# Second expert table of the last stage loaded in pieces of 512 rows by 512 columns, and six row buffers

## The chip, the core and the metric

One NeuronCore of one Trainium2 chip runs the whole program. The engines are TensorE (PE, matrix products), VectorE (DVE), ScalarE (ACT), GpSimd (POOL) and SyncE (SP), which work at the same time and wait for each other through semaphores. 16 DMA engines move data between HBM and the on-chip memory; SP issues the plain transfers, POOL the gathers by index. The metric is the time of one execution in microseconds, median of the runs.

## What is computed

One step of a decoder layer for 1024 prompt tokens and 64 sample tokens: three attention-like branches, then a layer of product-key experts (PEER), then a norm. The last stage concerns PEER alone: 16384 experts, each a row of 1024 values in the tables `peer_u` and `peer_v`; each token uses 8 x 16 of them.

```python
def peer_ffn(xn, w_pq, k1, k2, u_tab, v_tab):
    ...
    eidx = jnp.take_along_axis(cidx, pos, axis=-1)
    g = jax.nn.softmax(sc, axis=-1)
    ...
        a = jax.nn.gelu(jnp.einsum('td,thkd->thk', xb, u_tab[ib]).astype(jnp.float32))
        return jnp.einsum('thk,thkd->td', (gb * a).astype(v_tab.dtype), v_tab[ib])
```

All inputs and outputs are float32.

## The kernel before

The tokens are nine blocks of up to 128 (eight of the prompt, number 8 with the 64 sample tokens). Each block's experts are computed in one of two ways.

*Gathered blocks* (0 to 3, 6 and 7; `peer_gather`). For each of the 128 experts of a token POOL issues a gather of one row per token, 128 rows of 4 KB, 512 KB together, into a row buffer: 128 gathers of U rows (L1097) and 128 of V rows (L1108) for a block. DVE multiplies a U row with the token and sums (L1099, two instructions on DVE), and adds a weighted V row to the block's sum (L1114). U rows of head h+1 come before V rows of head h. The row buffers are taken in turn by `big`, and a gather waits until the row that last lay in its buffer is used up. In the last stage there are `ROWS2` of them: `ROWS` = 4 that are always there, and the others in the pool `dn` of the last stage.

*Dense blocks* (4, 5 and the sample block 8, 320 tokens together; `peer_dense`). Both tables are read whole, in 16 groups of DG = 8 slices of 128 experts. For each slice the U rows are loaded (L1218, 512 KB, tile `dur`), transposed on PE (L1223), split in a high part (ACT, L1225, `duh`) and a low part (DVE, L1226, `dul`), and 24 products of 320 columns give the activations (L1244 to L1247, `pa`). They become expert weights by a gelu and a product with the choice of each token (L1251, tile `c8`), and are split again (`dwh` on L1254, `dwl` on L1255). When a group's eight slices are done, eight *turns* follow, one for each 128 of the 1024 output columns: the V values of 1024 experts by 128 columns are loaded (L1259, 512 KB, tile `dvr`, two buffers), split (`dvh` on ACT, L1262; `dvl` on DVE, L1263), multiplied in 24 products (L1267 to L1269, `py`), and added to the sum `yT` on DVE (L1273). There are twelve weight buffers (DW), so that slices of the next group can run beside the turns of this one.

The gathers of blocks 6 and 7 run in the same stage as the dense blocks. The order of each engine's instructions is made when the program is built, by a list scheduler that goes by priorities and its own estimate of times; the gathers have the lowest priority and fill what it takes for gaps. On the chip this order is fixed: an engine waits at an instruction until its inputs are there. After the last turn each dense block is transposed back and normed (`finish`), and block 7 is finished when its last V row is added.

The functions that the change touches, and what calls them:

## Time and profile before

| | |
|---|---|
| median of 3 runs | 4262.14 us (4254.17 to 4282.94) |
| profiled execution | 4270.01 us, its span 4268.2 us |
| PE busy | 3480.7 us (82% of the span) |
| DVE busy | 3300.5 us (77%) |
| POOL busy | 2053.5 us (48%) |
| ACT busy | 1513.1 us (35%) |
| DMA | 1285.50 MB, mean 301 GB/s |
| gathers issued by POOL | 768 of U rows, 768 of V rows |

Busy time counts the stretches in which an engine had an instruction running; products on PE are pipelined, and their ends are modelled. In names of the trace the tiles of the last stage begin with d (`dvr`, `dur`, `duh`), and `in_peer_v_dram` is the V table in HBM. A wait is put down to what came last. PE's granted clock is given as a share of 2.4 GHz, and 0.5 is its lower level of 1.2 GHz.

### The profile page before, as it was taken

Reading aid. Unit: us, or ns where it says so; the run is one execution under the profiler, and the core shown is the slowest. Engines: PE = TensorE matmul, PEld = TensorE weight load, DVE = VectorE, ACT = ScalarE, POOL = GpSimd, SP = SyncE. Lnnn points to the kernel's source line nnn. Section 1 sums busy time; section 2 is a strip of 40 time slices with the busy share of each in tenths; the row PEclk is TensorE's granted clock in tenths of the full one; section 3 lists DMA queues with packets and bytes.
Section 4 is the critical chain, followed back from the end, with each engine's and each line's share of the span. In section 5 each row is a group of like instructions: output and inputs, shape, how many; then the busy total and the mean of one; then the engine's idle time right before and its main releaser. Section 6 shows DMA issues by size and latency. Waiting matters only on the chain.

```text
span 4268.2 us, 57773 instructions
## 1 busy us (share of the span) xinstructions
PE 3480.7 (82%) x19287; PEld 2867.8 (67%) x19287; DVE 3300.5 (77%) x7763; ACT 1513.1 (35%) x3138; POOL 2053.5 (48%) x1722
## 2 busy tenths in 40 slices
PE   4999895879967698587878877675589999898884
PEld 4989694656645557365655554453589999898884
DVE  3444368787787789888886656679999998898898
ACT  2565542324244112244464422111533333332331
POOL 0000003556656555665665667564344554555556
PEclk9999897989969898787888998887799999999997
DMA  3334346989989999898998899998899999999998
GB/s 114 109 96 146 122 158 205 321 287 344 368 278 372 361 354 312 308 321 283 365 322 312 329 328 353 381 370 304 323 348 331 341 357 357 359 355 363 335 353 300
DMA packets 690128, 1285.50 MB, mean 301 GB/s; under 512 B 66685, under 2 KB 447509, under 8 KB 687270
## 3 DMA queue, kind: packets, MB, share of 16 engines
q0 software_dynamic: 230480, 839.23, 53.4%
q1 hardware_dynamic: 459350, 442.58, 31.7%
q8 instruction: 153, 2.51, 0.2%
q14 instruction: 145, 1.19, 0.1%
HBM read 1213.04 MB, written 68.59 MB: 300 GB/s over the span
## 4 chain that ended last, share of the span: by engine, by line
PE 31%; DVE 16%; DMA 10%; issue 8%; ACT 3%; POOL 3%; another core or an unknown queue 1%; SPq 0%; POOLq 0%; DVEq 0%; ACTq 0%
DVE u L1099 5%; PE pj L272 4%; DVE acc L1114 4%; PE pa L1244 2%; PE pa L1245 2%; PE py L1269 2%; PE pj L275 2%; PE pa L1247 2%; PE py L1267 2%; PE py L1268 2%; DMA dvr<-in_peer_v_dram 2%; PE pt L1223 2%; DMA u<-in_peer_u_dram,ei 1%; POOL u L1097 1%; DMA v<-in_peer_v_dram,ei 1%
## 5 line engine op out<-in xcount | busy, mean ns | idle before, releaser
L1097 POOL DMA_INDIRECT u<-in_peer_u_dram,ei x768 | 972.2, 1266 | 796.9 <-DVE a L1099 191.5
L1108 POOL DMA_INDIRECT v<-in_peer_v_dram,ei x768 | 944.4, 1230 | 726.7 <-DVE acc L1114 285.2
L1114 DVE SCALAR_TENSOR_TENSOR acc<-v,a,acc 128x1024 f32<-128x1024 f32 x762 | 978.4, 1284 | 22.0 <-DMA v<-in_peer_v_dram,ei 14.6
L1099 DVE CUSTOM_DVE_ANT_0 u<-u,x 128x1024 f32<-128x1024 f32 x768 | 924.4, 1223 | 65.4 <-DMA u<-in_peer_u_dram,ei 61.7
L272 PE MATMUL pj<-aT,wr 128*128 128x384 f32 (+1 forms) x1664 | 530.4, 473 | 13.3 <-issue 5.2
L272 PEld LDWEIGHTS pj<-aT,wr 128*128 128x128 f32 x1664 | 317.6, 196 | 179.5 <-issue 19.6
L1267 PE MATMUL py<-dwh,dvh 128*128 128x320 f32 x1024 | 329.7, 324 | 55.1 <-ACT dwh L1254 32.3
L1269 PE MATMUL py<-dwh,dvl 128*128 128x320 f32 x1024 | 331.2, 324 | 42.7 <-DVE dvl L1263 42.7
L275 PE MATMUL pj<-wr,aT 128*128 128x256 f32 x1344 | 318.6, 395 | 22.5 <-DVE z L920 17.3
L1268 PE MATMUL py<-dwl,dvh 128*128 128x320 f32 x1024 | 328.1, 321 | 0.0
L1244 PE MATMUL pa<-xh,duh 128*128 128x320 f32 x1024 | 309.5, 315 | 6.6 <-ACT duh L1225 4.8
L275 PEld LDWEIGHTS pj<-wr,aT 128*128 128x128 f32 x1344 | 261.4, 198 | 65.4 <-DVE z L920 18.9
L1245 PE MATMUL pa<-xl,duh 128*128 128x320 f32 x1024 | 304.9, 310 | 0.0
L1225 ACT ACTIVATE duh<-pt 128x512 fp32r<-128x512 f32 x256 | 148.2, 597 | 382.9 <-PE pt L1223 347.0
L1267 PEld LDWEIGHTS py<-dwh,dvh 128*128 128x128 f32 x1024 | 203.4, 199 | 58.1 <-ACT dwh L1254 32.6
L1269 PEld LDWEIGHTS py<-dwh,dvl 128*128 128x128 f32 x1024 | 203.0, 198 | 49.0 <-DVE dvl L1263 49.0
L281 DVE TENSOR_TENSOR wl<-wr,wh 128x512 fp32r<-128x512 f32 x200 | 137.8, 691 | 123.3 <-PE pj L291 42.5
L1268 PEld LDWEIGHTS py<-dwl,dvh 128*128 128x128 f32 x1024 | 203.4, 199 | 0.3 <-DVE dwl L1255 0.3
L1244 PEld LDWEIGHTS pa<-xh,duh 128*128 128x128 f32 x1024 | 192.5, 188 | 11.2 <-ACT duh L1225 8.5
L1247 PE MATMUL pa<-xh,dul 128*128 128x320 f32 x1024 | 195.7, 320 | 0.0
L1245 PEld LDWEIGHTS pa<-xl,duh 128*128 128x128 f32 x1024 | 192.7, 188 | 0.0
L1226 DVE TENSOR_TENSOR dul<-pt,duh 128x512 fp32r<-128x512 f32 x256 | 171.9, 689 | 19.5 <-ACT duh L1225 17.4
(503 smaller groups left out, 7067.7 us busy)
## 6 DMA issues: line engine op xcount, KB each, us to landing
wr<-in_w_in_dram SPq DMA_DIRECT2D x168, 512.0 KB
dvr<-in_peer_v_dram SPq DMA_DIRECT2D x128, 512.0 KB
dur<-in_peer_u_dram SPq DMA_DIRECT2D x128, 512.0 KB
wr<-in_w_pq_dram SPq DMA_DIRECT2D x48, 512.0 KB
dc<-c_scr SPq DMA_DIRECT2D x15, 1280.0 KB
c_scr<-stg SPq DMA_DIRECT2D x16, 1024.0 KB
wr<-in_w_out_dram SPq DMA_DIRECT2D x24, 512.0 KB
u<-in_peer_u_dram,ei POOLq DMA_INDIRECT x768
```

Of the source, the lines that this page charges most:

```text
L272: PE.matmul(ps, raw[:, i, cols[0] * 128:cols[0] * 128 + 128], x[:, k], start=k == 0, stop=k == kt - 1)
L275: PE.matmul(ps, x[:, k, :], raw[:, i], start=k == 0 and first, stop=k == kt - 1 and last)
L1097: G.indirect_dma_start(out=r, out_offset=None, in_=UR, in_offset=bass.IndirectOffsetOnAxis(ap=ei[:, s:s + 1], axis=0))
L1099: V.tensor_tensor_reduce(r, r, x2, 1.0, 0.0, OP.mult, OP.add, a[:, s:s + 1])
L1108: G.indirect_dma_start(out=r, out_offset=None, in_=VR, in_offset=bass.IndirectOffsetOnAxis(ap=ei[:, s:s + 1], axis=0))
L1114: V.scalar_tensor_tensor(acc, r, a[:, s:s + 1], acc, op0=OP.mult, op1=OP.add)
L1244: PE.matmul(pa[:, :NT], uh[:, k], xh[:, k], start=k == 0, stop=False)
L1245: PE.matmul(pa[:, :NT], uh[:, k], xl[:, k], start=False, stop=False)
L1247: PE.matmul(pa[:, :NT], ul[:, k], xh[:, k], start=False, stop=k == 7)
L1267: PE.matmul(py[:, :NT], vh[:, j], wh, start=j == 0, stop=False)
L1268: PE.matmul(py[:, :NT], vh[:, j], wl, start=False, stop=False)
L1269: PE.matmul(py[:, :NT], vl[:, j], wh, start=False, stop=j == DG - 1)
```

## The change

The V table comes in pieces of 512 experts by 512 columns (tile `v4`, 1 MB, three buffers). Two pieces, of the first and of the last four slices, serve four turns; they are loaded at turns 0 and 4. A turn splits its 128 columns out of both pieces, with two instructions of half the size on ACT and on DVE each. A run of consecutive bytes in a load is 2 KB instead of 512 bytes. The tile `vr` is left with one buffer, for the end of the dense blocks. The last stage has six row buffers instead of eight.

```diff
--- before.py
+++ after.py
@@ -37,7 +37,7 @@
 OFF = [sum(NB[:a]) for a in range(16)]
 NCAND = sum(NB)
 
-ROWS, MORE, ROWS2 = 4, 3, 8
+ROWS, MORE, ROWS2 = 4, 3, 6
 SAMPLE = 8
 GROUPS = [[0, 1, 2], [3, 4, 5], [SAMPLE, 6, 7]]
 
@@ -1180,7 +1180,7 @@
 
 
         pd = ctx2.enter_context(tc.tile_pool(name="pd", bufs=1, space=bass.MemoryType.PSUM))
-        DB = {"ur": 3, "uh": 2, "ul": 2, "w": 4, "wh": DW, "wl": DW, "c": 2, "hot": 7, "eg": 1, "vr": 2, "vh": 2, "vl": 2}
+        DB = {"ur": 3, "uh": 2, "ul": 2, "w": 4, "wh": DW, "wl": DW, "c": 2, "hot": 7, "eg": 1, "v4": 3, "vr": 1, "vh": 2, "vl": 2}
         PB = {"t": 2, "a": 2, "y": 2, "c": 2}
 
         def DT(tag, shape, dt=F32):
@@ -1255,12 +1255,19 @@
                 V.tensor_tensor(wl, w, wh.bitcast(F32), op=OP.subtract)
                 W.append((wh, wl))
             for dt_ in range(8):
-                v = DT("vr", [128, DG, 128])
-                SP.dma_start(v, VR[g * DG * 128:(g + 1) * DG * 128, dt_ * 128:(dt_ + 1) * 128].rearrange(
-                    "(j p) d -> p j d", p=128))
+
+                if dt_ % 4 == 0:
+                    v4 = [DT("v4", [128, DG // 2, 512]) for _ in range(2)]
+                    for i, v in enumerate(v4):
+                        r = (g * DG + i * DG // 2) * 128
+                        SP.dma_start(v, VR[r:r + DG * 64, dt_ * 128:dt_ * 128 + 512].rearrange(
+                            "(j p) d -> p j d", p=128))
                 vh, vl = DT("vh", [128, DG, 128], F32R), DT("vl", [128, DG, 128], F32R)
-                A.activation(vh, v, AF.Copy)
-                V.tensor_tensor(vl, v, vh.bitcast(F32), op=OP.subtract)
+                for i, v in enumerate(v4):
+                    js = slice(i * DG // 2, (i + 1) * DG // 2)
+                    x = v[:, :, dt_ % 4 * 128:dt_ % 4 * 128 + 128]
+                    A.activation(vh[:, js], x, AF.Copy)
+                    V.tensor_tensor(vl[:, js], x, vh[:, js].bitcast(F32), op=OP.subtract)
                 py = DP("y")
                 for j in range(DG):
                     wh, wl = W[j]
```

The order of instructions changes with it, in the last stage alone. Two places show it.

On DVE, at the end of the dense blocks. Before, from the second-last update of `yT` on (L1273; L1114 adds a V row of block 7, L1073 and L1079 finish a dense block):

```order
L1273 TENSOR_TENSOR yT<-yT,py_34528 128x320
L1114 SCALAR_TENSOR_TENSOR acc_22963<-v_23595,a_22860,acc_22963 128x1024
L1114 SCALAR_TENSOR_TENSOR acc_22963<-v_23598,a_22860,acc_22963 128x1024
L1273 TENSOR_TENSOR yT<-yT,py_34560 128x320
L1114 SCALAR_TENSOR_TENSOR acc_22963<-v_23601,a_22860,acc_22963 128x1024
L1073 TENSOR_TENSOR dvr_34588<-dvr_34588,dur_34589 128x1024
L1114 SCALAR_TENSOR_TENSOR acc_22963<-v_23604,a_22860,acc_22963 128x1024
L1073 TENSOR_TENSOR dvr_34611<-dvr_34611,dur_34612 128x1024
L1114 SCALAR_TENSOR_TENSOR acc_22963<-v_23607,a_22860,acc_22963 128x1024
L1079 SCALAR_TENSOR_TENSOR dvr_34588<-dvr_34588,fr_34606,dur_34586 128x1024
```

Behind the last of these updates stand 15 instructions of L1114 in all, and none of L1099. With the change, from the second-last update of `yT` on, which is L1280 there:

```order
L1280 TENSOR_TENSOR yT<-yT,py_34656 128x320
L1114 SCALAR_TENSOR_TENSOR acc_22963<-v_23256,a_22860,acc_22963 128x1024
L1280 TENSOR_TENSOR yT<-yT,py_34688 128x320
L1102 TENSOR_TENSOR a_22860<-a_22860,gw_21819 128x16
L1114 SCALAR_TENSOR_TENSOR acc_22963<-v_23259,a_22860,acc_22963 128x1024
L1073 TENSOR_TENSOR dvr_34716<-dvr_34716,dur_34717 128x1024
L1114 SCALAR_TENSOR_TENSOR acc_22963<-v_23262,a_22860,acc_22963 128x1024
L1114 SCALAR_TENSOR_TENSOR acc_22963<-v_23265,a_22860,acc_22963 128x1024
L1114 SCALAR_TENSOR_TENSOR acc_22963<-v_23268,a_22860,acc_22963 128x1024
L1079 SCALAR_TENSOR_TENSOR dvr_34716<-dvr_34716,fr_34734,dur_34714 128x1024
L1114 SCALAR_TENSOR_TENSOR acc_22963<-v_23271,a_22860,acc_22963 128x1024
L1114 SCALAR_TENSOR_TENSOR acc_22963<-v_23274,a_22860,acc_22963 128x1024
```

Behind the last update there now stand 79 V rows (L1114) and 48 U rows (L1099, 96 instructions); ahead of it, from the first expert weight on, stand 181 U rows and 177 V rows, which were 224 and 240.

On SP, in the middle of the stage, the loads of U slices (`dur`, L1218) and of the V table before (`dvr`, L1259):

```order
L1218 DMA dur_26760<-in_peer_u_dram 128x1024
L1259 DMA dvr_26452<-in_peer_v_dram 128x8x128
L1218 DMA dur_26810<-in_peer_u_dram 128x1024
L1259 DMA dvr_26484<-in_peer_v_dram 128x8x128
L1235 DMA dc_27366<-c_scr 128x20x128
L1218 DMA dur_26860<-in_peer_u_dram 128x1024
L1259 DMA dvr_26516<-in_peer_v_dram 128x8x128
L1218 DMA dur_26910<-in_peer_u_dram 128x1024
L1259 DMA dvr_26548<-in_peer_v_dram 128x8x128
```

and with the change (a piece `v4` is printed as `dv` with a number, L1263):

```order
L1263 DMA dv_5949_27143<-in_peer_v_dram 128x4x512
L1263 DMA dv_5962_27274<-in_peer_v_dram 128x4x512
L1218 DMA dur_27092<-in_peer_u_dram 128x1024
L1218 DMA dur_27408<-in_peer_u_dram 128x1024
L1218 DMA dur_27458<-in_peer_u_dram 128x1024
L1218 DMA dur_27508<-in_peer_u_dram 128x1024
L1235 DMA dc_28072<-c_scr 128x20x128
L1218 DMA dur_27558<-in_peer_u_dram 128x1024
L1218 DMA dur_27608<-in_peer_u_dram 128x1024
L1263 DMA dv_5963_27275<-in_peer_v_dram 128x4x512
L1263 DMA dv_6049_27808<-in_peer_v_dram 128x4x512
```

Where a V load stood behind nearly every U load, two pieces of 1 MB now stand together after two to five U loads. At the stage's start three pieces stand ahead of the U loads, where two loads of `dvr` stood.

## Rows read from the trace of the kernel before

**Rows 1.** The page's head, its first part (busy time, share of the span and number of instructions of each engine) and, from the part with the costliest groups, four of them: line, engine, operation, out<-in with shapes, count | busy us, mean ns of one | idle time before and what ended it.
```profile
span 4268.2 us, 57773 instructions
PE 3480.7 (82%) x19287; PEld 2867.8 (67%) x19287; DVE 3300.5 (77%) x7763; ACT 1513.1 (35%) x3138; POOL 2053.5 (48%) x1722
...
L1097 POOL DMA_INDIRECT u<-in_peer_u_dram,ei x768 | 972.2, 1266 | 796.9 <-DVE a L1099 191.5
L1108 POOL DMA_INDIRECT v<-in_peer_v_dram,ei x768 | 944.4, 1230 | 726.7 <-DVE acc L1114 285.2
L1114 DVE SCALAR_TENSOR_TENSOR acc<-v,a,acc 128x1024 f32<-128x1024 f32 x762 | 978.4, 1284 | 22.0 <-DMA v<-in_peer_v_dram,ei 14.6
L1099 DVE CUSTOM_DVE_ANT_0 u<-u,x 128x1024 f32<-128x1024 f32 x768 | 924.4, 1223 | 65.4 <-DMA u<-in_peer_u_dram,ei 61.7
```

**Rows 2.** Busy time by stretch: from:to in us, length, then busy us and number of instructions of PE, PE's weight loads, DVE, ACT and POOL, then granted clock of TensorE, busy share of the DMA engines and GB/s.
```profile
3104.00:4230.00 1126.00, 1032.31 (x6966) 1014.16 (x6966) 1036.19 (x1755) 378.88 (x652) 584.47 (x468) 0.95 0.98 350
4230.00:4268.00 38.00, 1.56 (x10) 0.93 (x10) 28.47 (x24) 6.76 (x12) 17.72 (x16) 0.56 0.62 208
3150.00:3400.00 250.00, 242.66 (x1685) 239.01 (x1684) 245.76 (x586) 93.95 (x160) 116.81 (x91) 0.99 0.98 342
3600.00:4230.00 630.00, 549.23 (x3616) 537.77 (x3614) 564.42 (x799) 189.38 (x321) 346.77 (x279) 0.92 0.98 353
4150.00:4230.00 80.00, 53.05 (x290) 50.51 (x288) 71.00 (x88) 13.69 (x17) 57.38 (x45) 0.79 0.99 354
```

**Rows 3.** DVE in order of time at the end of the program: start us, us, line, operation, out<-in with shapes, how many in a row.
```profile
4229.57 0.49 DVE L1273 TENSOR_TENSOR yT<-yT,py 128x320 f32<-128x320 f32 x1 [0.95 <-PE py L1269]
...
4242.62 7.88 DVE L1114 SCALAR_TENSOR_TENSOR acc<-v,a,acc 128x1024 f32<-128x1024 f32 x6
...
4260.03 1.22 DVE L1073 TENSOR_TENSOR acc<-acc,h 128x1024 f32<-128x1024 f32 x1
```

**Rows 4.** What PE waited for from 3104 to 4230 us, the three largest: line, releaser: total us, times, longest us.
```profile
PE py L1269 <- DVE dvl L1263: 42.7, 21, 5.7
PE py L1267 <- ACT dwh L1254: 32.3, 1, 32.3
PE py L1267 <- ACT dvh L1262: 22.2, 8, 7.6
```

**Rows 5.** PE in order of time, at two places: start us, us, line, operation, and in brackets the idle time before it and what ended it. The first row is the first product with an expert weight, the two others are the first and the last of four products in a row at full clock.
```profile
3104.43 0.90 PE L1267 MATMUL py<-dwh,dvh 128*128 128x320 f32 x2 [32.30 <-ACT dwh L1254]
...
4139.51 0.31 PE L1268 MATMUL py<-dwl,dvh 128*128 128x320 f32 x1
...
4139.95 0.31 PE L1268 MATMUL py<-dwl,dvh 128*128 128x320 f32 x1
```

**Rows 6.** What ACT waited for from 3104 to 4230 us, one row.
```profile
ACT dvh L1262 <- DMA dvr<-in_peer_v_dram: 133.8, 32, 12.4
```

**Rows 7.** The chain of work that ended last, in order of time, one load of a V piece: start us, us, what.
```profile
3476.20 18.91 DMA dvr<-in_peer_v_dram
```

**Rows 8.** SyncE's queue in order of time, the two loads that it issued there.
```profile
3475.26 0.34 SPq L1218 DMA_DIRECT2D dur<-in_peer_u_dram  x1
3476.20 0.37 SPq L1259 DMA_DIRECT2D dvr<-in_peer_v_dram  x1
```

**Rows 9.** Busy time from 3104 to 4230 us of the instructions of one line alone (same columns as in group 2, for the engines that have any), for L1099 (u rows, two instructions each), L1114 (v rows) and L1223 (transposes of the U table).
```profile
3104.00:4230.00 1126.00, 271.29 (x448) 0.95 0.98 350
3104.00:4230.00 1126.00, 307.16 (x240) 0.95 0.98 350
3104.00:4230.00 1126.00, 138.21 (x952) 116.11 (x952) 0.95 0.98 350
```

**Rows 10.** DMA queues from 3100 to 4200 us: packets, MB, and the time that their packets took as a share of 16 engines over the stretch. q0 carries the gathers that POOL issues, q1 what SyncE issues.
```profile
q0 software_dynamic: 64811, 236.01, 56.9%
q1 hardware_dynamic: 181809, 147.87, 40.9%
```

**Rows 11.** Groups of instructions of the whole span (columns as in group 1): the two conversions of a V piece, their counterparts of half the size in an earlier stage, and the second instruction of a u row.
```profile
L1263 DVE TENSOR_TENSOR dvl<-dvr,dvh 128x1024 fp32r<-128x1024 f32 x128 | 156.3, 1223 | 32.4 <-ACT dvh L1262 31.7 <-issue 0.5
L281 DVE TENSOR_TENSOR wl<-wr,wh 128x512 fp32r<-128x512 f32 x200 | 137.8, 691 | 123.3 <-PE pj L291 42.5 <-PE cw L291 31.0 <-PE pj L299 22.6
L1262 ACT ACTIVATE dvh<-dvr 128x1024 fp32r<-128x1024 f32 x128 | 134.8, 1055 | 143.1 <-DMA dvr<-in_peer_v_dram 133.8 <-issue 4.9 <-PE py L1268 4.3
L279 ACT ACTIVATE wh<-wr 128x512 fp32r<-128x512 f32 x200 | 125.3, 630 | 141.9 <-PE pj L288 37.0 <-PE pj L296 33.5 <-PE cw L288 21.4
L1099 DVE DVE_READ_ACCUMULATOR2_ANT a<- 128x1 f32 x768 | 66.3, 86 | 0.0
```

**Rows 12.** The chain of work at the end of the program: start us, us, what.
```profile
4225.58 0.44 PE pt L1282 x4
...
4247.66 7.65 DMA v<-in_peer_v_dram,ei
```

**Rows 13.** POOL in order of time near the end of the program: one gather that waited for its row buffer.
```profile
4210.91 1.88 POOL L1108 DMA_INDIRECT v<-in_peer_v_dram,ei  x1 [0.59 <-DVE acc L1114]
```

**Rows 14.** POOL in order of time in an earlier stretch in which gathers of v rows follow each other: the first and the last of nine.
```profile
1214.10 1.03 POOL L1108 DMA_INDIRECT v<-in_peer_v_dram,ei  x1 [0.19 <-issue]
...
1226.93 0.94 POOL L1108 DMA_INDIRECT v<-in_peer_v_dram,ei  x1 [0.30 <-issue]
```

## The prediction

> **What bounds the kernel now.** The change touches only the last stage, and the instruction orders of the two kernels are the same up to it, so I read that stage alone. First the page: 4268.2 us of span, PE busy 82% and DVE 77% of it, none full over the whole [rows 1]. Then the busy time by stretch [rows 2]. The dense part runs from the first expert weight at 3104 us to the last update of yT at 4230 us (the start of that update, 4229.57, is in [rows 3]): 1126 us, in which PE is busy 1032 us, DVE 1036 us and the DMA engines 0.98 of the time. Three resources are almost full, so the question is which is late at the points where PE stands still. The waits of PE answer that [rows 4]: besides 32.3 us for the first dwh, which end at 3104.43 [rows 5] and so lie before the stretch, the largest are 42.7 us for dvl and 22.2 us for dvh, the two halves of a V piece. One step further back, ACT waited 133.8 us for the DMA of dvr [rows 6], and the chain shows one such load at 18.91 us from issue to landing for 512 KB [rows 7]. While PE waits, its clock also falls: granted 0.99 of full in 3150 to 3400, 0.92 from 3600 on, 0.79 in the last 80 us, where the V turns of the last group run with no U work left to cover them [rows 2]. So V loads cost time twice.
>
> The rows of the gather blocks are the other half. DVE takes 224 u rows (448 instructions, two per row) and 240 v rows inside the dense part [rows 9], and only 15 v rows are left behind it: the two workloads end together, 38 us apart [rows 2, 3]. Where a row is taken is fixed by DVE's static order, not by whether its data is there, and this decides the forecast.
>
> **The change, part by part.**
>
> *V pieces.* 128 loads of 512 KB in runs of 512 bytes become 64 of 1 MB in runs of 2 KB: 131072 runs become 32768. From the two queues' rows, 56.9% of 16 x 1100 us over 64811 packets is 154.5 ns for 3641 bytes, and 40.9% over 181809 is 39.6 ns for 813 bytes [rows 10]; a line through both leaves 6.6 ns per packet besides its bytes, so the saving is 98304 x 6.6 ns / 16 = 41 us of DMA time. More matters in who gets served. In the 18.91 us load a U load of 512 KB was issued 0.94 us ahead on the same queue [rows 7, 8], so 1 MB came in 19.9 us, 53 GB/s, while the engines moved about 350 GB/s [rows 2]: the gather queue took the rest. If the two queues alternate packet by packet, each engine serves 64 runs of 512 bytes with a gather packet between them: 64 x (154.5 + 27.4) ns = 11.6 us, plus 8 U packets x (154.5 + 173) ns = 2.6 us, 14.2 us, of the observed size. A new 1 MB piece has 32 runs of 2048 bytes: 32 x (154.5 + 90) ns = 7.8 us for twice the data. If shares went by bytes instead, a 1 MB piece would take about twice a present load: the first rival's case.
>
> *Its buffers.* Each half group needs two pieces and there are three buffers, so the second piece can only be issued when the first piece of the previous half is used up. SP issues in order: behind that waiting piece stand the U loads. Counted in the changed order, at the trace's durations, the DVE work that stands between a buffer's release and its next use is some 7 to 16 us for every second reload and over 25 us for the others, against 7.8 us plus a U load ahead. At the stage's start three pieces (3 MB) now go out ahead of the U loads instead of two loads of 512 KB, some 6 us at 350 GB/s; PE's wait of 32.3 us for the first dwh covers them. I take the V waits as gone, but for the small ones that the stretch 3150 to 3400 has too.
>
> *Split conversions.* DVE: 128 x 1223 ns become 256 of half size; the nearest rows of that size are 691 ns on DVE and 630 ns on ACT [rows 11]. That adds 128 x 0.16 = 20 us on DVE and 128 x 0.2 = 26 us on ACT. ACT is busy 379 of 1126 us, so nothing there. On DVE 106 fewer rows (below) at 1.25 us leave the dense part by the same change [rows 9]: 1036 - 132 + 20 = 924 us, hidden under PE. Without those fewer rows the 20 us would be on the path.
>
> *Dense part.* In 3150 to 3400 the present kernel runs 1685 matmuls in 250 us, at clock 0.99. The dense part has 6966 [rows 2]; at that pace 1034 us, so it ends at 4138 instead of 4230: 92 us gained. Bounds: the PE steps alone, 6014 products at 0.147 us and 952 transposes at 0.11 us [rows 5, 9, 12], are 989 us (4093); no gain at all is 4230.
>
> *Six row buffers, and where the rows stand.* In the changed order the dense part holds 181 u and 177 v rows instead of 224 and 240. Behind the last update of yT stand 48 u and 79 v rows, 127 instead of 15. Nothing can bring them forward: DVE's order is fixed. In that tail only the gather runs, and a row costs the slowest of: DVE 1.223 + 0.086 us for u and 1.284 for v [rows 1, 11]; POOL's issue, 1.266 (u) and 1.230 (v) plus the 0.30 us between two issues [rows 1, 14]; the ring of six, 0.59 + 1.87 us to issue, 7.65 - 1.0 to land and 1.3 to use, 10.4 / 6 = 1.74 us at the slowest [rows 12, 13]. POOL's step is confirmed by a stretch where it issues without waiting for rows: eight steps in 12.83 us, 1.60 us each [rows 14]. I take POOL's mean, 1.57 (u) and 1.53 (v): 48 x 1.57 + 79 x 1.53 = 196 us, less six rows already in their buffers (9), 187. Added are the last landing (6.6), its row (1.3), the end of block 7 from 4260.0 to 4268.2 (8.2) [rows 1, 3], and POOL's small instructions for the three dense blocks (5): 208 us, where the tail now takes 38. Bounds: 1.295 us a row (DVE's alone) gives 179 us in all, 1.78 us (45 POOL instructions in the crowded last 80 us [rows 2]) gives 236.
>
> **Sum.** 4268.2 - 92 + (208 - 38) = 4346, 78 us more than the span of the profiled execution. That execution's own time is 4270.0 and the median of the runs 4262.1, so the forecast for the median is 4262 + 78 = 4340 us, +1.8%. The gain in the dense part is real; the tail gives back more.
>
> **Rivals.**
> 1. *The V pieces stay late* (three buffers for pairs, shares by bytes). The second reload of each pair then lands after its 7 to 16 us, and the dense part keeps half its waits: 46 us more, 4386. For it: the short covers. Against: the packet counts. Chance 0.14.
> 2. *Six buffers starve the tail.* At 1.78 us a row the tail is 236 us: 4368. For it: ring and POOL limits lie within 0.2 us of each other. Against: the present tail takes six rows back to back in 7.88 us [rows 3]. Chance 0.12.
> 3. *Not slower* (the other side). PE near its floor and the tail at DVE's pace: the dense part ends at 4110, the tail takes 179: 4289, or 4283 as a median. It decides once dense end and tail together stay under 4311: with 4138 that is a row under 1.25 us, less than DVE's own 1.295, so both must come in low. Chance 0.11.
> 4. *Every issue in its long form.* A gather that starts when DVE has just freed its buffer, and goes on to the next row, took 0.59 + 1.88 us [rows 13], twice the 0.94 to 1.03 us of the short form [rows 14]. If all 121 gathers of the tail went so, 2.47 us each, the tail would take 320 us: 4452. The Trainium skill ("SBUF — State Buffer", section "SBUF: two separate sides") says that DVE and GpSimd share one pair of ports as an exclusive lock, held for a whole instruction by whoever comes first, for a DVE instruction with two inputs where the GpSimd one reads SBUF; by that rule an issue that meets a row waits for its end, and the trace agrees in the long form alone. Against: the means of 1.23 and 1.27 us over 768 gathers each, most of them beside a busy DVE [rows 1]. Chance 0.04.
> 5. *The DMA bound is lifted and nothing else moves.* The Trainium skill ("DMA: Bandwidth & Descriptors", section "Measured (HBM→SBUF, 128 partitions, SWDGE, issued from GpSimd)") advises transfers of at least 1 MiB, which the new pieces are. As a mechanism here: a stage bound by DMA at 0.98 ends 41 us earlier with the packets saved [rows 2, 10], 4221, if the rows stay beside the dense work. Against: the order puts 127 rows behind it. Chance 0.03.
>
> **Chances.** Forecast 0.56, rivals 0.14, 0.12, 0.11, 0.04, 0.03. Range 4290 to 4410: below lies most of rivals 3 and 5, above rival 4 and rival 1 together with a slow tail. About 1% (4219 to 4305) is what a measurement of this kernel can tell from no change: faster 0.03, same 0.11, slower 0.86.
>
> **What would show it.** Right: PE's waits for dvl and dvh fall from 65 us to under 25; granted clock above 0.97 in the dense part; last yT near 4138; then some 200 us in which PE does nothing and POOL issues a row every 1.5 to 1.6 us. Wrong: waits for the V DMA as long as now (rival 1); DVE in the tail waiting for u and v at 1.75 us a row (rival 2); rows going back to back at 1.3 us (rival 3). The forecast falls if the dense part ends before 4100 or the tail takes under 170 us.

## The result, and the profile after

| | before | after |
|---|---|---|
| median, same chip | 4264.47 us (4254.17 to 4282.94, 4 runs) | 4312.72 us (4299.94 to 4315.94, 4 runs) |
| ratio | | 1.0111, 95% interval 1.0072 to 1.0151 |
| profiled execution, span | 4270.01, 4268.2 us | 4299.94, 4298.1 us |

The changed kernel is 1.1% slower: 48 us by the medians, where 78 were forecast, and inside the range. Below, the *dense part* reaches from the start of the first product of `dwh` and `dvh` (the first with an expert weight) to the start of the last one, and the *tail* from there to the end of the span (that last start lies less than 1 us ahead of the last update of yT, which closed the stretches of [rows 2]); both together are the *stage*.

First the busy time by stretch of the changed kernel, dense part and tail, columns as in [rows 2]:

```profile
3077.00:4082.00 1005.00, 991.84 (x6957) 985.03 (x6958) 914.52 (x1727) 397.67 (x774) 417.60 (x358) 1.00 0.92 334
4082.00:4298.00 216.00, 4.40 (x21) 2.88 (x19) 171.29 (x192) 8.22 (x17) 154.88 (x132) 0.51 0.89 319
```

Against [rows 2] the dense part is 119 us shorter (1124.5 to 1005.3), the tail 177 us longer (39.3 to 215.8), the stage 57 us longer (1163.8 to 1221.1). The reader is to see three things in the first row: the granted clock is 1.00 in place of 0.95; DVE has 121 us less to do; and PE, with the same products, is busy 992 us instead of 1031 and stands still for 13 us of the stretch.

What PE waited for inside the dense part, and ACT's row on the V loads (line, releaser: us, times, longest), against [rows 4] and [rows 6]:

```profile
PE pt L1223 <- DVE dul L1226: 4.0, 4, 1.8
PE pa L1244 <- ACT duh L1225: 3.4, 2, 1.8
PE py L1274 <- ACT dvh L1269: 2.3, 2, 1.4
...
PE py L1276 <- DVE dvl L1270: 1.0, 2, 0.7
```
```profile
ACT dvh L1269 <- DMA dv<-in_peer_v_dram: 25.0, 11, 10.3
```

The two halves of V kept PE waiting 65 us and now 3; ACT waited 134 us for V's loads and now 25.

In the tail PE does nothing and POOL issues one gather after the other. POOL in order of time (start us, us, what, idle before), the first and the last of 26 gathers:

```profile
4129.99 0.95 POOL L1097 DMA_INDIRECT u<-in_peer_u_dram,ei  x1 [0.31 <-issue]
...
4146.55 1.87 POOL L1108 DMA_INDIRECT v<-in_peer_v_dram,ei  x1 [2.56 <-DVE acc L1114]
...
4169.33 1.98 POOL L1097 DMA_INDIRECT u<-in_peer_u_dram,ei  x1 [0.30 <-issue]
```

25 steps in 39.3 us are 1.57 us a row. From 4100 to 4270 us POOL waited for a row to be used up only 9 times, 8.8 us in all (the second row shows the longest), so its own issue is the pace; the gathers' queue meanwhile fills 91.5% of the DMA engines, which are therefore not far behind. Of the 124 gathers that it issues in the tail, 24 took over 1.5 us (two of them above); the mean is 1.22 us, and 0.30 us lie between two.

One difference between the two profiles is not the change's. The first product with an expert weight comes at 3077 us, at 3104 before ([rows 5]). 17 us of that are there before the last stage begins (the last product on L947 starts at 2918.2 us, before at 2935.7), where the orders of the two kernels are the same; and over the fourteen profiles of this study the product starts anywhere from 3053 to 3104 us, with old and with new loads of V. So profiles are compared by the stage alone below, and times by their ratios. A stage is that of one execution: against before, the stages of the table below and the ratios disagree by up to 28 us (e12: 45 us less by the stage, 17 by the ratio; e8: 18 more by the stage, 40 by the ratio), and a difference of 20 us between two profiles is not firm.

### The profile page after: what moved, and what is told of

It reads as the page before. It is cut to its first block, busy times and chain, and to the rows that moved or that the text cites. A ratio compares the mean times of both kernels' runs of the same rounds, so it can differ in the third digit from the quotient of the medians.

```text
span 4298.1 us, 57831 instructions
## 1 busy us (share of the span) xinstructions
PE 3424.7 (80%) x19287; PEld 2835.2 (66%) x19287; DVE 3315.1 (77%) x7891; ACT 1535.1 (36%) x3266; POOL 2013.7 (47%) x1722
## 4 chain that ended last, share of the span: by engine, by line
PE 35%; DVE 14%; DMA 9%; issue 7%; ACT 3%; POOL 3%; another core or an unknown queue 0%; SPq 0%; DVEq 0%; POOLq 0%; ACTq 0%
PE pj L272 5%; DVE u L1099 4%; PE pa L1244 3%; PE pa L1247 3%; PE pa L1245 3%; PE py L1275 3%; PE py L1274 3%; PE py L1276 3%; DVE acc L1114 3%; PE pt L1223 2%; PE pj L275 2%; POOL v L1108 1%; PE f L1370 1%; DMA v<-in_peer_v_dram,ei 1%; DMA u<-in_peer_u_dram,ei 1%
## 5 line engine op out<-in xcount | busy, mean ns | idle before, releaser
L1108 POOL DMA_INDIRECT v<-in_peer_v_dram,ei x768 | 911.8, 1187 | 799.5 <-DVE acc L1114 308.0
L1114 DVE SCALAR_TENSOR_TENSOR acc<-v,a,acc 128x1024 f32<-128x1024 f32 x762 | 974.7, 1279 | 37.1 <-DMA v<-in_peer_v_dram,ei 26.4
L1099 DVE CUSTOM_DVE_ANT_0 u<-u,x 128x1024 f32<-128x1024 f32 x768 | 922.3, 1217 | 81.6 <-DMA u<-in_peer_u_dram,ei 77.8
L1274 PE MATMUL py<-dwh,dvh 128*128 128x320 f32 x1024 | 315.7, 313 | 30.7 <-ACT dwh L1254 27.8
L1275 PE MATMUL py<-dwl,dvh 128*128 128x320 f32 x1024 | 316.7, 310 | 1.6 <-DVE dwl L1255 1.6
L1276 PE MATMUL py<-dwh,dvl 128*128 128x320 f32 x1024 | 313.2, 311 | 1.0 <-DVE dvl L1270 1.0
L1269 ACT ACTIVATE dvh<-dv 128x512 fp32r<-128x512 f32 x256 | 148.9, 625 | 237.1 <-PE py L1275 189.9
L1274 PEld LDWEIGHTS py<-dwh,dvh 128*128 128x128 f32 x1024 | 191.7, 189 | 32.1 <-ACT dwh L1254 28.1
L1275 PEld LDWEIGHTS py<-dwl,dvh 128*128 128x128 f32 x1024 | 192.9, 188 | 2.3 <-DVE dwl L1255 2.2
L1276 PEld LDWEIGHTS py<-dwh,dvl 128*128 128x128 f32 x1024 | 191.5, 188 | 2.0 <-DVE dvl L1270 1.7
```

The lines of the kernel that those rows point to most:

```text
L1099: V.tensor_tensor_reduce(r, r, x2, 1.0, 0.0, OP.mult, OP.add, a[:, s:s + 1])
L1108: G.indirect_dma_start(out=r, out_offset=None, in_=VR, in_offset=bass.IndirectOffsetOnAxis(ap=ei[:, s:s + 1], axis=0))
L1114: V.scalar_tensor_tensor(acc, r, a[:, s:s + 1], acc, op0=OP.mult, op1=OP.add)
L1274: PE.matmul(py[:, :NT], vh[:, j], wh, start=j == 0, stop=False)
L1275: PE.matmul(py[:, :NT], vh[:, j], wl, start=False, stop=False)
L1276: PE.matmul(py[:, :NT], vl[:, j], wh, start=False, stop=j == DG - 1)
```

## Experiments

Theory 1, with which they began, is the prediction's: the pieces bring V in time and so shorten the dense part, and the six buffers lengthen the tail, each on its own. Rival A: six buffers slow the rows on the chip itself. Rival B: it is the amount of V held ahead that counts, not the length of its runs. All kernels and what they gave, *V waits* being PE's waits for dvl and dvh in the dense part, *ACT on V* ACT's wait for V's loads, *rows* those in the dense part and in the tail by the order built:

| kernel | row buffers, V | rows | dense us | tail us | V waits | ACT on V | ratio to before (95%) |
|---|---|---|---|---|---|---|---|
| before | 8, 512 KB | 464, 15 | 1124.5 | 39.3 | 65 | 134 | |
| after | 6, pieces | 358, 127 | 1005.3 | 215.8 | 3 | 25 | 1.0111 (1.0072 to 1.0151) |
| e1 | 6, 512 KB | 382, 103 | 1034.1 | 176.8 | 14 | 105 | 1.0070 (1.0043 to 1.0098) |
| e9 | 7, 512 KB | 426, 55 | 1079.9 | 101.9 | 45 | 106 | 1.0040 (1.0017 to 1.0064) |
| e8 | 9, 512 KB | 478, 0 | 1162.6 | 19.5 | 95 | 149 | 1.0095 (1.0057 to 1.0132) |
| e13 | 12, 512 KB | 465, 0 | 1253.3 | 19.2 | 139 | 117 | 1.0268 (1.0233 to 1.0304) |
| e2 | 8, two pieces | 381, 99 | 1022.5 | 161.8 | 8 | 45 | 1.0054 (1.0025 to 1.0083) |
| e3 | 9, 256 columns | 381, 89 | 1029.7 | 154.5 | 6 | 0 | 1.0042 (1.0021 to 1.0062) |
| e12 | 12, 256 columns | 462, 0 | 1098.7 | 19.6 | 15 | 0 | 0.9960 (0.9936 to 0.9983) |
| e4 | as after, runs of 512 bytes | 360, 127 | 1017.9 | 209.8 | 1 | 23 | 1.0111 (1.0073 to 1.0149) |
| e5 | as before, runs of 4 KB | 464, 15 | 1103.8 | 39.3 | 53 | 66 | 0.9964 (0.9939 to 0.9989) |
| e6 | as before, 3 of 16 gathers out | 448, 28 | 1089.3 | 57.9 | 6 | 120 | 0.9968 (0.9945 to 0.9991) |
| e10 | as before, DVE's row work halved | 483, 0 | 1142.8 | 19.1 | 85 | 147 | 1.0017 (0.9991 to 1.0043) |
| e11 | e6, DVE's V sums halved | 475, 0 | 1081.0 | 19.1 | 35 | 87 | 0.9875 (0.9844 to 0.9907) |

(The rows of e6 and e11 are those that DVE works on; some 365 and 380 of them are transferred in the dense part. Where the order built has no row in the tail, some rows run ahead of the first product: e12 has 462 rows in its stage and before 479, so a part of e12's gain by the stage is rows that it did earlier.)

### One half of the change alone: six buffers (e1)

```diff
-ROWS, MORE, ROWS2 = 4, 3, 8
+ROWS, MORE, ROWS2 = 4, 3, 6
```

> The kernel before with one number changed, six row buffers in the last stage instead of eight; the table V is still loaded in blocks of 1024 rows by 128 columns. Theory 1 (the two halves of the change act apart: the pieces remove the waits for V, the six buffers move rows of the gathers behind the dense part, where POOL issues one in about 1.55 us): the waits for dvl, dvh and dvr stay as they were (PE some 65 us for dvl and dvh, ACT over 100 us for dvr), the order built has 103 rows in the tail instead of 15, 103 x 1.55 = 160 us there plus the end of 15 to 20 us, the dense part ends near 4215 us, and the run takes about 4390 us, 1.03 times the time before. Rival A (fewer buffers make the rows wait on the chip itself, for their transfers, and the place of the rows in the order counts for little): the dense part's rows wait for transfers, and the tail takes over 2.0 us a row, over 200 us, so 4430 us or more. Rival C (the rows that are left for the tail relieve the queues of the dense part, and V's waits fall by themselves): PE's waits for dvl and dvh under 30 us, the dense part ends near 4170 us, and the run takes about 4340 us.

Busy time of its dense part and tail, then PE's waits for V:

```profile
3071.00:4105.00 1034.00, 1002.99 (x6961) 992.33 (x6961) 938.36 (x1634) 380.30 (x650) 457.56 (x381) 0.99 0.97 337
4105.00:4282.00 177.00, 2.43 (x18) 1.56 (x16) 140.67 (x158) 7.29 (x15) 129.53 (x108) 0.51 0.89 320
```
```profile
PE py L1269 <- DVE dvl L1263: 7.2, 7, 1.7
PE py L1267 <- ACT dvh L1262: 6.5, 6, 2.7
```

This overturns the prediction's first step. With V still loaded in blocks of 512 KB, PE's waits for it fall from 65 to 14 us and the dense part by 90 us: Rival C of the expectation, and more than it had (a dense part that ends near 4170 and starts at 3104 takes 1066 us, and it took 1034). ACT still waits 105 us for its loads, but this lateness hardly reaches PE any more; rows that leave the dense part take work from VectorE's order and bytes from the queues there, and this run does not part the two. The tail, 103 rows, is where all theories but A had it. By the ratios, 0.7 of the 1.1% are there with six buffers alone. The pieces on top of them (after against e1) take 29 us off the dense part and put 24 more rows, 39 us, behind it.

### The other half, with more buffers (e2, e3)

e2 is the changed kernel with eight row buffers and two of the pieces:

```diff
-ROWS, MORE, ROWS2 = 4, 3, 6
+ROWS, MORE, ROWS2 = 4, 3, 8
...
-        DB = {"ur": 3, ..., "v4": 3, "vr": 1, "vh": 2, "vl": 2}
+        DB = {"ur": 3, ..., "v4": 2, "vr": 1, "vh": 2, "vl": 2}
```

e3, against the kernel before, takes pieces of 1024 rows by 256 columns, converted whole, and `ROWS2` 9; its core:

```diff
-                v = DT("vr", [128, DG, 128])
-                SP.dma_start(v, VR[g * DG * 128:(g + 1) * DG * 128, dt_ * 128:(dt_ + 1) * 128].rearrange(
-                    "(j p) d -> p j d", p=128))
...
+                if dt_ % 2 == 0:
+                    v4 = [DT("v4", [128, DG, 256])]
...
+                        SP.dma_start(v, VR[r:r + DG * 128, dt_ * 128:dt_ * 128 + 256].rearrange(
+                            "(j p) d -> p j d", p=128))
```

> The changed kernel with eight row buffers, paid for by a piece buffer (two of the pieces instead of three). 99 rows in the tail instead of 127. Theory 1 (POOL's issue of 1.55 us a row sets the tail's length, and the pieces alone keep V on time): 28 rows fewer behind the dense part, 28 x 1.55 = 43 us, so about 4265 us if two piece buffers are enough for V to come in time, waits for dvl and dvh under 10 us. Rival A (it is the transfers that starve with six buffers): eight buffers also shorten each row in the tail, below 1.45 us, so 4250 us or less. Rival B (V's waits went because three pieces of 1 MB are held ahead, not because of the piece's shape): with two, PE waits over 30 us for dvl and dvh, and the time is 4300 us or more.

> V in pieces of 1024 rows by 256 columns (1 MB, runs of 1 KB), each used for two turns, converted whole as in the kernel before; two buffers, one of which also takes the rows of the last combination, so that nine row buffers fit. 89 rows in the tail. Theory 1: V comes in time with runs of 1 KB too, the waits for dvl and dvh stay under 10 us, the tail takes 89 x 1.55 = 138 us plus about 15, and the run takes about 4245 us, less than either kernel. Rival B (it is the amount held ahead that counts, 2 MB here against 3 MB in the changed kernel and 1 MB before): PE waits 20 to 40 us for dvl and dvh, 4275 us. Rival D (only runs of 2 KB get V through beside the gathers): PE waits over 50 us, 4300 us or more.

Both have V on time (8 and 6 us of waits), a dense part of 1022 to 1030 us and a tail shorter than the changed kernel's by what its rows cost. They are still slower than before by 0.5 and 0.4%, a miss for e3, which was to beat both kernels; Rivals B and D, with 20 us of waits or more in e3, did not come. Against e1, with as many rows beside the dense work, the pieces are worth 12 and 4 us of dense part: little, because there e1's short blocks are nearly on time too. The tails of before, after, e1 to e4 and e9 follow 19.4 us + 1.53 us a row within 10 us; the five kernels with no row there have tails of 19.1 to 19.6 us. e2's rows, 1.44 us each, are just under the limit set for Rival A, but e3's with nine buffers are at 1.52 and e1's with six at 1.53: the number of buffers does not set a row's time.

### The length of the runs (e4, e5)

e4 loads each piece of the changed kernel by four transfers of 128 columns:

```diff
-                        SP.dma_start(v, VR[r:r + DG * 64, dt_ * 128:dt_ * 128 + 512].rearrange(
-                            "(j p) d -> p j d", p=128))
+                        for q in range(4):
+                            SP.dma_start(v[:, :, q * 128:q * 128 + 128],
+                                         VR[r:r + DG * 64, (dt_ + q) * 128:(dt_ + q) * 128 + 128].rearrange(
+                                             "(j p) d -> p j d", p=128))
```

e5 leaves the kernel before as it is and reads 4 KB rows into the same tiles:

```diff
-                SP.dma_start(v, VR[g * DG * 128:(g + 1) * DG * 128, dt_ * 128:(dt_ + 1) * 128].rearrange(
-                    "(j p) d -> p j d", p=128))
+                SP.dma_start(v.rearrange("p j d -> p (j d)"), VR[(g * DG + dt_) * 128:(g * DG + dt_ + 1) * 128, :])
```

> The changed kernel, its pieces, buffers and order of rows, except that each piece of 512 rows by 512 columns is loaded by four transfers of 128 columns, so in runs of 512 bytes as in the kernel before. Theory 1 (V was late because its short runs share the queues with the gathers run by run, and the change helps by runs of 2 KB): the loads take several times as long, the waits for V come back, PE waits 40 to 90 us for dvl and dvh and the run takes 4350 to 4400 us. Rival B (V is on time because three pieces are held ahead, whatever their runs): waits for dvl and dvh under 10 us, and the time within 10 us of the changed kernel's.

> The kernel before with its tiles, its buffers and its order of instructions (464 rows in the dense part, 15 behind it), except that each block of V is read as 128 whole rows of 1024 columns, so in runs of 4 KB in place of 512 bytes: the same number of bytes, but other elements of V, so y of the dense blocks is another result. It parts the length of the runs from everything else. Theory 1 (V is late because of its short runs): the waits for dvl and dvh fall under 15 us, the dense part takes about 1035 us instead of 1124, and the time is about 85 us below before, ratio 0.98. Theory 2, formed after the first four runs (the dense part of before is bound by its DMA engines, 98% busy at 350 GB/s, and V's waits are only the place where that shows; the changed kernel's dense part is shorter because 106 rows left it): the same bytes have to come, so the dense part takes 1080 to 1125 us, PE or DVE goes on waiting for V or for rows, and the ratio is 0.99 to 1.0.

Of e4, PE's waits for V; of e5, the busy time of the dense part, PE's waits for V, and the queue of SyncE's transfers from 3100 to 4200 us as in [rows 10]:

```profile
PE py L1276 <- ACT dvh L1271: 0.8, 1, 0.8
PE py L1278 <- DVE dvl L1272: 0.5, 1, 0.5
```
```profile
3103.00:4207.00 1104.00, 1027.45 (x6962) 1013.30 (x6963) 1034.62 (x1751) 377.59 (x650) 576.98 (x466) 0.96 0.96 357
```
```profile
PE py L1268 <- DVE dvl L1262: 41.1, 17, 5.7
...
PE py L1266 <- ACT dvh L1261: 11.4, 4, 4.5
```
```profile
q1 hardware_dynamic: 72784, 148.92, 36.7%
```

e4 is Rival B's case: with runs of 512 bytes V is as punctual as in the changed kernel, and the time is the same. e5 shows what long runs are worth by themselves where 464 rows stand beside them: 0.36%, 21 us of stage, as Theory 2 had it. ACT's wait for the loads halves (134 to 66 us), but 53 us of PE's V waits are left. The DMA time saved is what the prediction's price gives: 40.9% of 1100 us ([rows 10]) less 36.7% is 46 us, and 6.6 ns for each of the 109025 packets fewer are 45. It became 21 us of time.

### How many rows, how many buffers (e6, e8, e9)

e8 and e9 are the kernel before with nine and seven row buffers (`ROWS2`, the line of e1's diff). e6 keeps its eight and leaves out three gathers of sixteen:

```diff
-                r = big("u")
-                G.indirect_dma_start(out=r, out_offset=None, in_=UR,
-                                     in_offset=bass.IndirectOffsetOnAxis(ap=ei[:, s:s + 1], axis=0))
+                if b not in LATER or k % 5 != 4:
+                    r = big("u")
+                    G.indirect_dma_start(out=r, out_offset=None, in_=UR,
+                                         in_offset=bass.IndirectOffsetOnAxis(ap=ei[:, s:s + 1], axis=0))
```

(and the same for v).

> The kernel before with eight row buffers and its short runs of V, but in blocks 6 and 7 three gathers of sixteen are left out (VectorE takes the row before once more, so its work stays, and y of these blocks is another result): about 365 rows are transferred beside the dense part, as many as in the changed kernel. Theory 2 (the number of rows beside the dense part decides, not the pieces and not the number of buffers): the dense part takes 1010 to 1040 us instead of 1124, PE waits under 20 us for dvl and dvh, DMA is at most 97% busy, and the time is about 4150 to 4180 us. Theory 1 (runs of 512 bytes stay late beside gathers): the waits for dvl and dvh stay above 40 us and the dense part takes 1080 us or more. Rival A (it was the six buffers that made room): as Theory 1.

> The kernel before with nine row buffers; the order built has every row in the dense part (478, none behind it). Theory 2 (a row behind the dense part costs about 1.56 us, one beside it 1.1 to 1.5 us of DMA time): 15 rows off the tail save 23 us, and cost 16 to 22 us in the dense part, so 0 to 7 us faster, ratio 0.998 to 1.0. Theory 1 (a row in the dense part costs only what it delays V): 10 to 20 us faster, ratio 0.995 to 0.998. If a ninth row in flight makes V later still: the waits for dvl and dvh rise from 65 to over 90 us, and the run is no faster.

> The kernel before with seven row buffers; 426 rows in the dense part, 55 behind it, between before and e1_rows6. Theory 2 (dense part bound by DMA above some 385 rows, 1.1 to 1.5 us a row): the dense part takes 1067 to 1082 us, the tail 39 + 40 x 1.56 = 101 us, together 1168 to 1183 us against 1164 before, ratio 1.001 to 1.005. Theory 1 in its other form (V comes in time as soon as the queues are a little less full): the waits for dvl and dvh fall below 20 us at once, the dense part takes about 1035 us, and the run is some 25 us faster than before, ratio 0.994.

The dense parts of e6, e8 and e9, and the three largest waits of PE in e6's:

```profile
3095.00:4184.00 1089.00, 1019.72 (x6959) 998.41 (x6959) 1013.55 (x1774) 381.62 (x652) 453.78 (x365) 0.97 0.92 313
```
```profile
3096.00:4259.00 1163.00, 1045.73 (x6961) 1025.64 (x6962) 1054.12 (x1766) 380.25 (x653) 601.13 (x474) 0.94 0.96 343
```
```profile
3088.00:4168.00 1080.00, 1025.06 (x6960) 1009.36 (x6961) 990.58 (x1701) 378.26 (x653) 515.89 (x428) 0.97 0.98 345
```
```profile
PE pa L1246 <- ACT duh L1227: 26.6, 13, 12.5
PE pt L1225 <- DVE dul L1228: 18.1, 17, 2.6
PE py L1269 <- DVE yT L1275: 8.5, 4, 2.6
```

e9 came as Theory 2 (DMA as the bound) said. e6 did not: with as few transfers as the changed kernel and DMA at 92% the dense part is still 1089 us, not 1010 to 1040. V's own waits are gone there, and the conversions of U, which stand in the same queues of ACT and DVE, wait instead. e8 came as neither theory had it, but as the third case of its expectation: V came later still (95 us of waits), and 14 rows more beside the dense work cost 38 us there and saved 20.

### VectorE's work (e10, e11)

e10 halves DVE's two row operations (512 of 1024 columns) and leaves all transfers; e11 does so for the v rows on top of e6.

```diff
-                    V.scalar_tensor_tensor(acc, r, a[:, s:s + 1], acc, op0=OP.mult, op1=OP.add)
+                    w = 512 if b in LATER else 1024
+                    V.scalar_tensor_tensor(acc[:, :w], r[:, :w], a[:, s:s + 1], acc[:, :w], op0=OP.mult, op1=OP.add)
```

> The kernel before, its loads and its row transfers unchanged (eight row buffers), but in blocks 6 and 7 VectorE's product of a row and its sum of a row are done over 512 of the 1024 columns, so that y of these blocks is another result. VectorE has some 280 us less work, DMA the same; the order built has all 483 rows in the dense part, none behind it, so it is read against e8_rows9 (478 rows, dense part 1163 us, VectorE busy 1054 us). Theory 3, formed after the second batch (VectorE, 91 to 93% busy in the dense part of every kernel run so far, sets its pace with its turns to and from ScalarE; DMA at 96 to 98% stands close behind it): the dense part falls to what DMA allows, 403 MB at 350 to 365 GB/s, 1104 to 1150 us, or lower if the 98% are no limit, down to 1010 us. Theory 2 (DMA alone): 403 MB at 343 to 350 GB/s, 1150 to 1175 us, unchanged.

> As e6_drop (three of sixteen gathers of blocks 6 and 7 left out, which took the dense part only from 1124 to 1089 us), and VectorE's sum of a row done over 512 of the 1024 columns as well, so that VectorE has some 160 us less to do. y of these blocks is another result. Theory 3 (VectorE's work held e6_drop at 1089 us): the dense part falls to TensorE's own pace, 1005 to 1025 us, and the time to about 4140 us. Rival E (it is the steps from engine to engine and the place of the rows in the order, not VectorE's work): the dense part stays above 1070 us.

Their dense parts:

```profile
3085.00:4228.00 1143.00, 1041.96 (x6960) 1021.14 (x6961) 824.19 (x1774) 379.95 (x654) 504.64 (x479) 0.95 0.97 353
```
```profile
3053.00:4134.00 1081.00, 1023.36 (x6962) 1005.24 (x6963) 925.30 (x1802) 381.36 (x654) 455.09 (x383) 0.97 0.92 325
```

Theory 3 (VectorE's work sets the pace) falls. e10 takes 230 us of work from DVE against e8 and gains 20 us of dense part; e10's 1143 us lie within the theory's bounds for DMA, but e11 has less of both (DVE 925 us, 88 less than e6 where 160 were expected) and stays at 1081, Rival E's case. What e10 and e11 keep is the late V: ACT waits 147 and 87 us for its loads, PE 85 and 35 us for the two halves.

### The pieces with every row beside the dense work (e12, e13)

e12 is e3 with more row buffers, paid for elsewhere; e13 has the same three numbers in the kernel before, with V's loads and buffers as they were there.

```diff
-ROWS, MORE, ROWS2 = 4, 3, 9
+ROWS, MORE, ROWS2 = 4, 3, 12
...
-DG, DW = 8, 12
+DG, DW = 8, 8
...
-        DB = {"ur": 3, ..., "hot": 7, ...}
+        DB = {"ur": 3, ..., "hot": 4, ...}
```

> A version meant to beat both kernels: V in pieces of 1024 rows by 256 columns (runs of 1 KB), two buffers, converted whole; twelve row buffers, paid for with fewer buffers of the expert weights (eight pairs instead of twelve) and of the one-hot tables; the order built has all rows of this stage in the dense part, none behind it. Theory 3: VectorE has as much to do in the dense part as in e5_runs4k (464 rows, 1104 us with long runs), the tail falls from 39 to 20 us, together 1125 to 1140 us against 1164 before: 25 to 40 us faster, ratio 0.991 to 0.994. Against it: with eight pairs of weights each group of experts starts only as the last products of the one before end, and a stall of 2 us or more at each of 16 groups eats the gain: ratio 1.0 or more, and TensorE waits over 30 us for dwh. As in e8_rows9 (nine rows in flight, 18 us slower in this stage than before), more rows in flight can also make V and the rows late: then waits for dvh and dvl of 60 us or more.

> e12_256r12 with V loaded as in the kernel before (blocks of 1024 rows by 128 columns, runs of 512 bytes, two buffers of 512 KB): twelve row buffers, eight pairs of weights, all 465 rows in the dense part and none behind it, as in e12_256r12 (462 rows, stage 1118 us from the first product with an expert's weights to the end, PE waits for dvh and dvl 15 us). It parts the pieces from all else at one number of rows. If the pieces do it (V held further ahead, in longer runs, comes in time although every row is beside it): here dvh and dvl keep PE waiting 50 to 100 us, as in before and e8_rows9, the dense part takes 1125 to 1160 us, and the ratio to before is 0.998 to 1.005, against 0.996 for e12_256r12. If the number of bytes beside the dense part and its place in the order do it (DMA 96 to 98% busy, 343 to 357 GB/s in each of before, e5, e8, e10 and e12): the same 390 MB take the same 1095 to 1110 us, and the ratio is 0.994 to 0.997.

Dense part and tail of e12, then of e13, and the waits of PE for V in e13; last, what SyncE's queue in e13 and in e12 waited for most before it could issue a load of V, from 3110 to 4060 us:

```profile
3096.00:4194.00 1098.00, 1032.50 (x6958) 997.40 (x6958) 1031.94 (x1745) 378.01 (x651) 570.53 (x456) 0.98 0.96 353
4194.00:4214.00 20.00, 2.81 (x20) 1.93 (x18) 9.10 (x8) 5.59 (x10) 3.16 (x7) 0.68 0.31 105
```
```profile
3079.00:4332.00 1253.00, 1073.12 (x6959) 1042.04 (x6960) 1048.10 (x1752) 381.67 (x652) 592.26 (x458) 0.92 0.87 312
4332.00:4351.00 19.00, 2.73 (x19) 1.84 (x18) 7.91 (x7) 5.59 (x10) 3.07 (x6) 0.70 0.24 83
```
```profile
PE py L1269 <- DVE dvl L1263: 82.7, 32, 9.2
PE py L1267 <- ACT dvh L1262: 56.2, 22, 10.6
```
```profile
SPq L1259 <- DVE dvl L1263: 204.9, 49, 11.1
```
```profile
SPq L1263 <- DVE dvl L1270: 135.4, 32, 10.4
```

At one number of rows, of row buffers and of weights, the pieces are worth 154 us of stage (1118 against 1272), and by the ratios, 0.996 against 1.027, some 131 us. This is what Theory 1 had said of them, in a place where it holds: with some 460 rows beside the dense work, where e1 to e3 with 381 showed 4 to 12 us. No run has the pair with eight row buffers and twelve pairs of weights. e13's dense part was expected at 1125 to 1160 us and is slower still. e12 beats both kernels: 0.4% under before, and with the changed kernel at 1.0111 about 1.5% under it. It gains less than expected (0.991 to 0.994): PE waits 25 us for `dwh` inside the dense part, where the changed kernel shows none, the price of fewer weight buffers that its expectation had named.

## Why the prediction came out as it did

**V's waits vanish, and the clock recovers: right as an outcome, wrong in its cause.** The waits fell from 65 to 3 us (under 25 forecast) and the clock rose to 1.00 (above 0.97 forecast). But e1 gets most of that (14 us, 0.99) from six buffers alone, and e4 gets nearly all of it (1 us, 0.99) with the old runs. That the waits came out as forecast is therefore luck in part: the change holds a second cause, the rows taken away, for which the prediction had a term in DVE's work but none in V's waits. The step failed at "More matters in who gets served": runs that share the queues were to make V late. e5 has runs of 4 KB and keeps 53 us of V waits.

What the runs put in its place is in part shown and in part argued. The kernel before holds V only two turns ahead. In its trace a load goes out when the conversion `dvl` of two turns earlier has freed a buffer: the median time between the two is 0.0 us, and SyncE's queue waits before a V load for this more than for anything else (3110 to 4060 us):

```profile
SPq L1259 <- DVE dvl L1263: 148.9, 55, 5.8
```

From there to its own conversion a load has a median of 13.1 us. ACT had to wait for 33 loads: it stood ready for them a median of 7.9 us after their buffer was freed, and they took 5.4 to 22.0 us, a median of 9.8. Of these, 25 took less than 13.1 us and would have been in time with the usual lead; the other eight were long transfers. That a piece which serves two or four turns is asked for earlier, and so is on time, is argued from this; e12 against e13 shows the effect. That pair differs in the length of runs too, 1 KB against 512 bytes, and what of the 154 us is theirs was not measured apart.

Why V keeps PE waiting longer with more row buffers (14, 45, 65, 95 us at six, seven, eight and nine) stays open. The rows' work in DVE's order and their transfers grow together there, and the runs that part them fit neither: e10, with 211 us less of DVE's work than before and all transfers, keeps 85 us; e6, with nearly as much DVE work as before and 365 transfers, has 6; e11, with less of both, has 35.

**Dense part at 1034 us: the term that was mis-sized.** It took 1005, a gain of 119 us, not 92. The pace came from the stretch 3150 to 3400 us [rows 2], where rows and DMA at 0.98 stand beside the products: its 91 POOL instructions are 376 in 1034 us. That is e1's case, 382 rows and 1034 us, not the changed kernel's, with 24 rows fewer. PE's own steps were the lower bound, 989 us, and the truth lay nearer to that.

**Split conversions: right.** DVE's 914 us (924 forecast) and ACT's 398 (405) are hidden beside 992 us of PE.

**Tail of 208 us, set by POOL's issue: right.** 216 us, 1.57 us a row in the stretch shown, nearly all of them POOL's own steps. With 19.4 + 1.53 x rows over all tails this is the firmest number of the study.

**Sum.** +57 us of stage against +78, and +48 by the medians: the dense part came out some 27 us shorter than forecast, the tail 8 us longer. Rival 3 (not slower) did not come, since no tail of fifty rows or more came under 1.43 us a row. Rival 5's mechanism, fewer DMA microseconds and rows still beside the dense work, is e5: 15 us by its ratio, where the rival had 41. Rivals 1 and 2 have no trace in the profile. The long form of rival 4 is there in some of the gathers (1.87 and 1.98 us above), as it was before, but not in every one.

**The trade that decides the sign.** A row taken out of the dense part gives back 1.0 to 1.2 us (before to e9, 45 us for 38 rows; e9 to e1, 46 us for 44) and costs 1.53 us behind it. Above 464 rows it turned: e8 paid 38 us for 14 rows. Each figure is the difference of two profiles, but the ratios go the same way, lowest at eight buffers (1.0070, 1.0040, 1, 1.0095 for six to nine). The three pieces take 24 KB of each partition where two blocks took 8, and a row buffer is 4 KB: the change pays in row buffers for pieces that e1 shows to be hardly needed once those rows are gone. With pieces in place a row moved back beside the dense work costs 0.85 us there (e3 to e12, 69 us for 81 rows) and saves 1.5: pieces, there of 256 columns, gain once the memory comes from elsewhere.

**Still open.** e11 and e1 move the same bytes beside the dense part (351 and 349 MB) with DVE equally loaded (925 and 938 us), yet take 1081 and 1034 us. Number of row buffers and the place of the rows in the order differ, and no run parts the two. Why e13 is 91 us slower in its dense part than e8, which has more rows, was not parted either: twelve buffers, or fewer buffers of weights.

## What to carry to other kernels

When a load is late, look first at when it could be issued: if it waits for a buffer that an in-order engine frees late, more of it held ahead can help (here 4 to 12 us with 381 rows beside it, 131 to 154 with some 460), while longer runs alone helped little (21 us). Before paying for one stage with buffers of another, count where the build's order puts the other's work, and price a unit of it in both places (here 1.0 to 1.2 us beside the dense work up to 464 rows, 1.53 us behind it). Run each half of a change alone: the half that seemed the cost here, six buffers, did by itself most of what the other half was meant to do.

## What was not expected of the hardware

Where PE waits more, its products take longer too. For the same some 6960 products of the dense part it was busy 992 us at a mean granted clock of 1.00 (after), 1003 at 0.99 (e1), 1025 at 0.97 (e9), 1031 at 0.95 (before), 1046 at 0.94 (e8) and 1073 at 0.92 (e13), in the order of their V waits: 3, 14, 45, 65, 95 and 139 us. From after to e13 that is 81 us of slower products on 136 us more of V waits. It goes with PE's idle time as a whole (13, 31, 55, 93, 117 and 180 us) rather than with V: e6 and e12, with 6 and 15 us of V waits but 69 and 66 us of idle time, were busy 1020 us at 0.97 and 1033 at 0.98. The mean clock is not all of it, since e9 at 0.97 was busy 1025.

The time from issue to landing grows far less than the size: medians in 3110 to 4050 us, over the quarter to half of the loads whose landing the profile tells, were 7.2 us for 256 KB (e4), 8.9 us for 512 KB in runs of 512 bytes (e1), 9.5 us for 1 MB in runs of 1 KB (e3) and 11.1 us in runs of 2 KB (e2), all beside gathers. The single load of 18.91 us on which the prediction built its sharing of the queues [rows 7] was no typical one: the 33 late loads of the same kernel took a median of 9.8 us.
